# A gradient matmul on one core: three of the loads of G cut into 120 and 8 partitions

## The chip, the cores and the metric

The kernel runs on one core of a Trainium2 chip. The metric is the device time of one execution in microseconds (us), the median of several runs. A core has TensorE (PE, matmuls, with its weight loads shown as PEld), VectorE (DVE), ScalarE (ACT), GpSimd (POOL) and SyncE (SP), each working through its own instructions in order, and 16 DMA engines that move data between device memory and the core's on-chip memory of 128 partitions.

## The reference

```python
def reference(input, grad_output):        # input [16, 512, 1024] f32, grad_output [16, 512, 768] f32
    grad_weight = np.einsum('bmk,bmn->kn', input, grad_output)
    return grad_weight.astype(np.float32) # [1024, 768]
```

With batch and rows joined it is one product, X transposed times G, where X has 8192 x 1024 and G has 8192 x 768 elements.

## The kernel before

**Tiles.** The 8192 rows are cut into 64 slices of 128, and two slices make a pair `u`, from 0 to 31 (so the 5th, 9th and 13th pair are u = 4, 8 and 12). A pair's X is the tile `xp` (128 partitions, 2 x 1024, bf16), its G the tile `gp` (128 partitions, 2 x 768, bf16). The string `LOADS` (L12) gives each pair a kind. Kind `s` (the first seven and the last two pairs) gives two items that are multiplied plainly. Kind `P` (the 23 pairs between) gives one item for a scheme in the manner of Strassen, with seven products of half size in place of eight: DVE makes three sums of G halves (`ge`) and three of X halves (`xe`) and overwrites two halves of each tile in five instructions, `sum_g1` (L139), `sum_g2` (L144), `sum_x1` (L149), `sum_x2` (L153) and `sum_x3` (L158).

**Loads.** The loop at L108 to L126 issues all loads from POOL, in the order of the pairs. For u of 2 and above a pair is one transfer of G (L114) and one of X (L115). Both read f32 and write bf16. Partition p receives rows 2p and 2p + 1 of the pair, so each partition's data is one stretch of memory. The pairs live in 14 buffers (`PAIRS_HELD`), the sums in 9 (`SUMS_HELD`). POOL does nothing else; its queue holds just these transfers. The first two slices are loaded in f32 by SP and ACT and rounded there.

**Sums and products.** The output has quadrants A, B, C, D (each 512 x 384, as four blocks of 128 rows, q = 0 to 3). The five further products of the scheme are m, n, o, p and q. A product works in four banks of matmul memory, a slot; there are two slots, so two products are open at a time. A step such as `D9:2` in `ORDER` (L18 to L32) says: go on with product D up to its 9th item. A step with `!` closes the product afterwards: each bank is added to or copied into its sum in on-chip memory, by DVE (L356, L358), or by ACT (L354) for as many of the last banks as stand after the colon. ACT also carries a sum back into a bank before a product that it closes is opened again (L297, L324). The order on PE, DVE, ACT and POOL is the program's own order (`manual_schedule`, L84): `fill` hands out the DVE sums and, late in the kernel, the 20 `share` operations (L195) at the places that the numbers in `ORDER` name.

**What the steps around the loads need.** Products o and p read only halves that no sum overwrites, so their matmuls (L338) can begin when the pair's X and G have landed. q and n need `sum_x1` and `sum_g2`; m, D and A need other sums. The last P pair is u = 29, first used in step `5p23!1,0,1,1`. Pairs u = 30 and 31 are plain and used from `A38:0-q` on. The end, L389 to L403, stores the last block of D in two parts.

Of the kernel before, what the change touches and what calls it, by code (L numbers as in the profile page):

```python
# [9 lines left out]
P = 128  # L10
# [30 lines left out]
SUMS_HELD = 9  # L41

MERGED = 2


@with_exitstack
def kernel(
# [6 lines left out]
    nc = tc.nc  # L54
# [14 lines left out]
    G = grad_output.rearrange("b m n -> (b m) n")  # L69
# [38 lines left out]
    for u, kind in enumerate(LOADS):  # L108
        pool = pairs if u else head
        xp = pool.tile([P, 2, K], bf16, name="xp", tag="xp")  # L110
        gp = pool.tile([P, 2, N], bf16, name="gp", tag="gp")
        if u >= MERGED:
            rows = slice(2 * u * P, 2 * (u + 1) * P)
            nc.gpsimd.dma_start(out=gp, in_=G[rows, :].rearrange("(p m) n -> p m n", m=2))  # L114
            nc.gpsimd.dma_start(out=xp, in_=X[rows, :].rearrange("(p m) k -> p m k", m=2))  # L115
        for h in range(2):
            s = 2 * u + h
            if s > 0 and u < MERGED:
                nc.gpsimd.dma_start(out=gp[:, h, :], in_=G[s * P : (s + 1) * P, :])
            if s > 1 and u < MERGED:  # L120
                nc.gpsimd.dma_start(out=xp[:, h, :], in_=X[s * P : (s + 1) * P, :])
            if kind == "s":
                items.append(("s", xp[:, h, :], gp[:, h, :]))
        if kind == "P":
            items.append(("P", xp, gp))
        xg.append((xp, gp))  # L126
# [326 lines left out]
```

## Time and profile before

| | before |
|---|---|
| median of 3 runs | 162.97 us (162.89 to 163.16) |
| span of the profiled execution, first to last instruction | 161.1 us |
| PE busy | 157.0 us (97%) |
| DVE busy | 140.7 us (87%) |
| ACT busy | 117.9 us (73%) |
| POOL busy | 34.8 us (22%) |
| DMA queue of POOL's loads | 9360 packets, 28.64 MB written |
| read from device memory | 58.72 MB |

The times around the span (launch and end) are 1.87 us, the median less the span. Of the profile, the chain of work that ended last goes back from the last instruction to what released each; the groups give an operation's count, its busy time and the idle time before it with the releaser; the waits add up who waited for whom; the timeline lists instructions by start time, with the idle time before one and its releaser in brackets. "PEld" lines are weight loads, which run beside the matmul before them. A DMA transfer adds 16 to a count when it is done, one for each DMA engine, and the trace holds the time of each of the 16 increments and the queue, size and time of each DMA packet.

### The profile page before, as it was taken

Reading aid. Unit: us, or ns where it says so; the run is one execution under the profiler, and the core shown is the slowest. Engines: PE = TensorE matmul, PEld = TensorE weight load, DVE = VectorE, ACT = ScalarE, POOL = GpSimd, SP = SyncE. Lnnn points to the kernel's source line nnn. Section 1 sums busy time; section 2 is a strip of 40 time slices with the busy share of each in tenths; the row PEclk is TensorE's granted clock in tenths of the full one; section 3 lists DMA queues with packets and bytes.
Section 4 is the critical chain, followed back from the end, with each engine's and each line's share of the span. In section 5 each row is a group of like instructions: output and inputs, shape, how many; then the busy total and the mean of one; then the engine's idle time right before and its main releaser. Section 6 shows DMA issues by size and latency. Waiting matters only on the chain.

```text
span 161.1 us, 2769 instructions
## 1 busy us (share of the span) xinstructions
PE 157.0 (97%) x944; PEld 92.7 (58%) x944; DVE 140.7 (87%) x267; ACT 117.9 (73%) x278; POOL 34.8 (22%) x69
## 2 busy tenths in 40 slices
PE   8999999999999999999999999999999999999991
PEld 3365665556555565556655665556655665555561
DVE  0645888889799999999998999999989998999982
ACT  3735357545589899978998897997795667988730
POOL 7442222122222212222212222221222100000000
PEclk9999999999999999999999999999999999999999
DMA  5999999999999999999999999999999999900695
GB/s 176 297 210 214 213 214 216 212 215 212 214 213 212 212 212 216 212 213 211 214 212 217 212 215 213 213 213 213 213 212 213 213 214 213 202 21 0 239 354 191
DMA packets 12398, 33.40 MB, mean 207 GB/s; under 512 B 1376, under 2 KB 4192, under 8 KB 12384
## 3 DMA queue, kind: packets, MB, share of 16 engines
q0 software_dynamic: 9360, 28.64, 89.8%
q1 hardware_dynamic: 2592, 3.47, 6.2%
q10 hardware_dynamic: 432, 1.11, 1.8%
q8 instruction: 7, 0.11, 0.3%
q14 instruction: 7, 0.06, 0.1%
HBM read 58.72 MB, written 3.15 MB: 384 GB/s over the span
## 4 chain that ended last, share of the span: by engine, by line
PE 97%; DVE 0%; issue 0%
PE bank L338 94%; PE bank L97 3%; PE bank L393 0%; DVE acc L401 0%
## 5 line engine op out<-in xcount | busy, mean ns | idle before, releaser
L338 PEld LDWEIGHTS <-xp 128*128 128x128 bf16 x650 | 63.3, 98 | 44.4 <-DVE xp L212 1.5
L338 PE MATMUL bank<-gp,xp 128*128 128x384 bf16 x468 | 81.0, 327 | 0.0
L354 ACT COPY macc<-bank 128x384 f32<-128x384 f32 x91 | 39.3, 491 | 9.8 <-PE bank L338 9.4
L358 DVE TENSOR_TENSOR acc<-bank,acc 128x384 f32<-128x384 f32 x80 | 39.6, 550 | 5.2 <-PE bank L338 4.8
L338 PEld LDWEIGHTS <-xe 128*128 128x128 bf16 x276 | 26.9, 98 | 17.9 <-DVE xe L149 0.2
L354 ACT COPY acc<-bank 128x384 f32<-128x384 f32 x57 | 24.7, 484 | 13.9 <-PE bank L338 13.9
L297 ACT COPY bank<-macc 128x384 f32<-128x384 f32 x73 | 33.0, 493 | 1.6 <-DVE acc L358 0.9
L338 PE MATMUL bank<-ge,xp 128*128 128x384 bf16 x182 | 33.5, 326 | 0.0
L338 PE MATMUL bank<-gp,xe 128*128 128x384 bf16 x184 | 32.4, 326 | 0.0
L297 ACT COPY bank<-acc 128x384 f32<-128x384 f32 x47 | 21.5, 491 | 8.7 <-DVE acc L358 7.0
L115 POOL DMA_DIRECT2D xp<-in_input_dram x30 | 16.0, 532 | 52.1 <-DMA xp<-in_input_dram 28.9
L114 POOL DMA_DIRECT2D gp<-in_grad_output_dram x30 | 16.0, 533 | 38.1 <-PE bank L338 17.2
L358 DVE TENSOR_TENSOR macc<-bank,macc 128x384 f32<-128x384 f32 x35 | 18.0, 550 | 0.8 <-PE bank L338 0.8
L139 DVE TENSOR_TENSOR ge<-gp 128x1152 bf16<-128x1152 bf16 x23 | 17.3, 752 | 0.6 <-DMA gp<-in_grad_output_dram 0.5
L149 DVE TENSOR_TENSOR xe<-xp 128x1024 bf16<-128x1024 bf16 x23 | 15.8, 685 | 2.1 <-DMA xp<-in_input_dram 2.1
L195 DVE TENSOR_TENSOR acc<-acc,macc 128x768 f32<-128x768 f32 (+1 forms) x20 | 16.1, 871 | 0.0
L338 PE MATMUL bank<-ge,xe 128*128 128x384 bf16 x92 | 15.9, 326 | 0.0
L158 DVE TENSOR_TENSOR xp<-xp 128x1024 bf16<-128x1024 bf16 x23 | 15.7, 684 | 0.0
L144 DVE TENSOR_TENSOR gp<-gp 128x768 bf16<-128x768 bf16 x23 | 12.7, 554 | 0.5
L153 DVE TENSOR_TENSOR xe<-xp 128x512 bf16<-128x512 bf16 x23 | 9.6, 418 | 0.0
L356 DVE COPY acc<-bank 128x384 f32<-128x384 f32 x6 | 3.2, 555 | 3.2 <-PE bank L338 3.1
L212 DVE CAST gp<-gf 128x192 bf16<-128x192 f32 (+1 forms) x2 | 0.7, 330 | 4.3 <-DMA gf<-in_grad_output_dram 4.3
(20 smaller groups left out, 19.9 us busy)
## 6 DMA issues: line engine op xcount, KB each, us to landing
xp<-in_input_dram POOLq DMA_DIRECT2D x30, 512.0 KB, 16.8
gp<-in_grad_output_dram POOLq DMA_DIRECT2D x30, 384.0 KB, 16.7
out_dram<-acc SPq DMA_DIRECT2D x15, 192.0 KB, 2.4
xf<-in_input_dram ACTq DMA_DIRECT2D x2, 512.0 KB, 4.8
gp<-in_grad_output_dram POOLq DMA_DIRECT2D x3, 192.0 KB, 6.4
xp<-in_input_dram POOLq DMA_DIRECT2D x2, 256.0 KB, 7.7
gf<-in_grad_output_dram SPq DMA_DIRECT2D x2, 192.0 KB, 4.2
out_dram<-acc SPq DMA_DIRECT2D x1, 128.0 KB, 1.9
```

The costliest lines, as they stand in the source:

```text
L114: nc.gpsimd.dma_start(out=gp, in_=G[rows, :].rearrange("(p m) n -> p m n", m=2))
L115: nc.gpsimd.dma_start(out=xp, in_=X[rows, :].rearrange("(p m) k -> p m k", m=2))
L139: nc.vector.tensor_add(out=ge.rearrange("p a n -> p (a n)"), in0=g[:, 0 : 3 * NH], in1=g[:, NH : 4 * NH])
L144: nc.vector.tensor_sub(out=g[:, 0::3, :], in0=g[:, 0::3, :], in1=g[:, 2:0:-1, :])
L149: nc.vector.tensor_add(out=xe[:, 0:2, :].rearrange("p a k -> p (a k)"), in0=xp[:, 0, :], in1=xp[:, 1, :])
L153: nc.vector.tensor_add(out=extra[i][0][:, 2, :], in0=xp[:, 0, 0:KH], in1=xp[:, 1, KH:K])
L158: nc.vector.tensor_sub(out=x[:, 1:3, :], in0=x[:, 1:3, :], in1=x[:, 0::3, :])
L195: op(out=dst, in0=dst, in1=src)
L297: nc.scalar.copy(out=bank, in_=sum_of(p, q))
L338: nc.tensor.matmul(bank, stat, mov, start=opening and j == 0 and not carried, stop=close and j == len(items_now) - 1, skip_group_check=car ...
L354: nc.scalar.copy(out=dst, in_=bank)
L358: nc.vector.tensor_add(out=dst, in0=bank, in1=dst)
```

## The change

```diff
+SPLIT = (4, 8, 12)
...
         if u >= MERGED:
             rows = slice(2 * u * P, 2 * (u + 1) * P)
-            nc.gpsimd.dma_start(out=gp, in_=G[rows, :].rearrange("(p m) n -> p m n", m=2))
+            gsrc = G[rows, :].rearrange("(p m) n -> p m n", m=2)
+            for r in (slice(0, 120), slice(120, P)) if u in SPLIT else (slice(0, P),):
+                nc.gpsimd.dma_start(out=gp[r], in_=gsrc[r])
             nc.gpsimd.dma_start(out=xp, in_=X[rows, :].rearrange("(p m) k -> p m k", m=2))
```

For pairs u = 4, 8 and 12 the transfer of G becomes two: first partitions 0 to 119, then partitions 120 to 127, both from POOL and both ahead of the pair's X. All other transfers, the bytes, and the instructions of PE, DVE, ACT and SP stay as they are in the program.

## The prediction

> **What bounds the kernel now.** I read the chain that ended last first, then the strip of slices, the groups, the waits, and then two narrow stretches of the timeline.
>
> ```profile
> PEclk9999999999999999999999999999999999999999
> DMA  5999999999999999999999999999999999900695
> GB/s 176 297 210 214 213 214 216 212 215 212 214 213 212 212 212 216 212 213 211 214 212 217 212 215 213 213 213 213 213 212 213 213 214 213 202 21 0 239 354 191
> ```
>
> ```profile
> 0.78 4.42 PE bank L97 x6
> 5.20 2.25 PE bank L338 x12
> 7.45 0.01 issue
> 7.46 149.34 PE bank L338 x914
> ```
>
> The chain is TensorE from end to end: 914 matmuls in 149.34 us, 163.4 ns each, at the full granted clock. The middle distance between two matmul starts in the trace is 162.5 ns, so all waiting inside this piece is 149.34 − 914 × 0.1625 = 0.8 us, and half of it lies before 16 us. A change can hardly shorten this chain; it can only put holes into it. The strip shows the second thing: the DMA engines are full from the second slice until 142 us, at 213 GB/s. So loads run at their own ceiling, and a load's landing time is set by the bytes in front of it on its engine, not by when POOL issues it.
>
> How near are the two to each other? The waits of the whole run and the timeline around the last pair of kind P (the 30th) say so:
>
> ```profile
> POOL xp L115 <- DMA xp<-in_input_dram: 28.9, 17, 2.0
> ...
> DVE xe L149 <- DMA xp<-in_input_dram: 2.1, 4, 0.8
> ...
> PEld L338 <- DMA xp<-in_input_dram: 0.5, 2, 0.3
> ```
>
> ```profile
> 132.32 2.78 PE L338 MATMUL bank<-gp,xp 128*128 128x384 bf16 x16
> ...
> 133.60 0.69 DVE L149 TENSOR_TENSOR xe<-xp 128x1024 bf16<-128x1024 bf16 x1 [0.41 <-DMA xp<-in_input_dram]
> 133.62 1.25 PEld L338 LDWEIGHTS <-xp 128*128 128x128 bf16 x9 [0.23 <-DMA xp<-in_input_dram]
> ```
>
> At 133.6 us both DVE and the weight load stand waiting for the 30th pair's X (step p23). The completion count of that transfer is full at 133.58 us and the matmul starts at 133.63: a slack of 0.05 us. The matmuls stream through the wait without a hole (the PE line has none), so it costs nothing today; but any later landing goes straight into TensorE. By the same reckoning (first matmul on a pair less the last of its X's 16 completion increments) the slack is 0.36 us for the 9th pair (43.21 us), 0.45 for the 14th (64.85), 0.5 for the 23rd (103.88).
>
> The 16 increments of a transfer, one per DMA engine, also show which engine decides. Up to 20 us all 16 come within 0.35 us. Then one engine after the other falls back by about 1 us and stays back, after one 16 KB packet of the instruction queue each (893 to 999 ns; at 20.8, 42.1, 63.2, 82.9, 104.8, 124.3 us). At the 30th pair's X seven engines are 0.97 to 1.31 us behind the first, and the landing is theirs.
>
> **The change, part by part.**
>
> *Issue.* Three more L114 transfers of 0.53 us (the row "530/530/587" of that line) are 1.6 us of POOL. Each also takes its turn in POOL's wait for the transfer eight places earlier:
>
> ```profile
> 7.62 0.54 POOL L115 DMA_DIRECT2D xp<-in_input_dram  x1 [2.02 <-DMA gp<-in_grad_output_dram]
> 8.53 0.53 POOL L114 DMA_DIRECT2D gp<-in_grad_output_dram  x1 [0.37 <-DMA gp<-in_grad_output_dram]
> 9.78 0.53 POOL L115 DMA_DIRECT2D xp<-in_input_dram  x1 [0.72 <-DMA xp<-in_input_dram]
> 10.73 0.53 POOL L114 DMA_DIRECT2D gp<-in_grad_output_dram  x1 [0.42 <-DMA gp<-in_grad_output_dram]
> ```
>
> The 5th pair's X (issued at 9.78) moves to the next such turn, about 10.7 us, and everything behind it one place. It landed at 25.6 us, so 15 us of queued transfers cover a shift of 1 us; later issues sit 16.8 us ahead (the median to landing), and one turn there is about 2.1 us. Cost 0; without that cover it would be up to 2.1 us a split.
>
> *Waits.* A reader of these three G's has one more transfer to wait for. TensorE's sequencer has 23 separate waits of 51 ns on L338 today without a hole at most of them, and DVE the same kind, so I bound it by 0 and 0.05 us for each of three pairs. Queued behind it are, for the 5th pair, the matmuls of D9 (26.5 us, with the data there 0.9 us before); for the 9th and 13th sum_g1 on DVE and the four sums behind it, which TensorE waits for (the 13th pair's xe was ready 0.06 us before its matmul at 61.43). I take 0.
>
> *Engine load.* This decides. A G transfer is 0.393 MB at 213 GB/s, 1.85 us; its 128 rows are 8 on each engine, so a row costs its engine 0.23 us. No row of this trace shows a transfer of 120 or of 8 partitions. Bounds: all eight rows on the one engine that the 120 leave out (or 120 spread 7 and 8, and the eight filling up): nothing changes; all eight on one engine that already had eight: +1.85 us there. Nearest row: every load in the trace is spread evenly over 16 engines, so I take 15 engines with 8 rows each, one engine with none, and the last eight rows on eight engines, one each. Then each split makes eight engines 0.23 us later for good (the queue never empties, so nothing is caught up), and one engine 1.85 or 1.62 us earlier, which helps nobody: a landing is the last engine's. Each extra transfer also adds one 4-byte completion of 22 ns to every engine.
>
> After three splits 24 rows lie on 16 engines: an engine has three of them if the eight are the same engines each time (0.69 + 0.07 = 0.76 us), two if they rotate (0.46 + 0.07 = 0.53 us). With seven engines sharing the last place at the 30th pair, one with two or three rows is nearly certain among them. The landing moves by 0.53 to 0.76 us, less the slack of 0.05: 0.48 to 0.71. I take 0.55, since the last increments differ by 0.3 us and the engine with most rows need not be the very last.
>
> *On the way.* The 9th pair's X is up to 0.5 us late against 0.36, and DVE, which waits for it at 42.86 (0.76 us), passes that on to 61.43, where 0.06 is left: 0.1 to 0.4 us of hole. The 14th is 0.5 to 0.8 late against 0.45. These holes come first and the later wait shrinks by as much: they aren't added, the largest lateness counts. After 133.6 us only about 0.1 us of TensorE waiting is left that could swallow some of it, and the last two pairs land at 137.9 and 142.2 us, 4.5 us and more before their matmuls (143.6 and 146.7).
>
> **Sum.** Span 161.1 + 0.55 = 161.65; the median of the runs, 162.97, is 1.87 above the profiled span, so 163.5 us, +0.33%.
>
> Two rules of the Trainium skill, DMA: Bandwidth & Descriptors, weigh in. The section "Why a DMA increments its semaphore by 16 and not by 1" says that the engines used are the largest number up to 16 that divides the outer dimension (or, for some GpSimd copies, sixteenths rounded up): 15 for 120 rows, eight for 8, which would make it 163.5 to 163.7. The table "Rules for kernel authors" says that two transfers to disjoint partitions share the same engines and bring nothing; by that alone it would be 163.0. The increments above show why "nothing" may be too kind here. The page also calls engines 7 and 15 usually slower, which would speak for relieving one engine; in this trace no engine falls back steadily, they step back one after the other.
>
> **Rivals.**
>
> *No change.* The eight rows fill the engine that was left out, or fall on engines that are not among the last seven, or the 120 are spread in a way that evens out; then the change does not do what it says. Only the 0.07 us of completions against 0.05 of slack remain: 163.0, up to 163.25 with one row on a late engine. For: DVE and TensorE wait little for loads today. Against: seven of sixteen engines share the last place.
>
> *Faster.* The engine that is left out is the last one: just after 23 us one engine alone is 1.26 us behind, and the 5th pair's G would bring it in front; landings up to 34 us come some 0.6 us earlier. It decides only where TensorE has a hole that a load ends. From 16 us to the end all its holes together are 0.4 us, and those at 26.8 and 42.3 us follow copies of ACT. Gain at most 0.2 us: 162.8; for more, the runs without profiler would have to have holes that this trace hasn't.
>
> *Much slower.* The eight rows go to one engine that already carries eight: 1.85 us for one such split among the late engines, 5.5 if it is the same engine three times: 164.8 to 168.4. For: eight rows is what an engine gets in every transfer of this trace. Against: the even spread.
>
> **How the numbers follow.** Forecast 163.3 to 163.8: 0.55. No change: 0.26. Faster mechanism: 0.07 (with something outside this trace). Much slower: 0.12. A difference of 0.2% (0.33 us) is about what a measurement of this kernel can tell from no change; the border lies at 163.30. Slower: 0.53 + 0.12 = 0.65; same 0.28; faster 0.07. The range leaves out the much slower case and the far end of the faster one: 162.8 to 164.2.
>
> **What would show it.** Right: the wait of the weight load for X at the last combined pair grows from 0.23 us to 0.7 or more, with a hole in the matmuls of the same size; DVE's waits for X (2.1 us in all) grow; landing increments of pairs after the 13th end 0.5 to 0.8 us later; matmul durations stay. Wrong: no such hole though landings are later (slack misread), landings not later (rows spread otherwise), or a hole right after the 5th, 9th or 13th pair that ends on an extra wait.

## The result, and the profile after

The changed kernel takes **163.79 us** (163.73 to 163.89), the kernel before 162.97 us (162.89 to 163.16); the ratio is 1.0043, 95% interval 1.0023 to 1.0064. A second series, with 23 runs of the kernel before beside it, gives 1.0035 (1.0022 to 1.0048), which is 0.57 us (0.36 to 0.78). The change makes the kernel slower by about 0.4%.

The strips of the changed kernel have the same shape: the TensorE clock is full to the end of the matmuls, and the DMA engines are full until about 143 us.

```profile
PEclk9999999999999999999999999999999999999998
DMA  5999999999999999999999999999999999900695
GB/s 158 300 212 213 212 217 211 213 211 211 216 212 212 213 213 212 213 211 214 212 214 214 213 214 211 215 212 213 211 212 215 211 215 206 191 16 0 219 357 203
```

The chain that ended last is what differs (start, length, what). Before it was one unbroken row of matmuls; now it leaves TensorE at 79.7 us, runs through DVE and two loads of X, and comes back to TensorE at 134.64 us, after a load:

```profile
7.85 71.87 PE bank L341 x438
79.72 0.53 DVE macc L361
...
82.61 17.22 DMA xp<-in_input_dram
99.85 0.69 DVE xe L152
...
117.63 16.96 DMA xp<-in_input_dram
134.59 0.05 issue
134.64 23.17 PE bank L341 x141
```

The load issued at 117.63 us is the X of the 30th pair, the place that the prediction named. The chain counts that load from its issue, but the issue did not make it late: the first DMA engine was through with it at 127.41 us and the last at 134.59. The waits of the run (who, for whom, us in total, times, longest) and the timeline there:

```profile
DVE xe L152 <- DMA xp<-in_input_dram: 2.2, 5, 0.6
...
DVE ge L142 <- DMA gp<-in_grad_output_dram: 1.3, 4, 0.5
...
PEld L341 <- DMA xp<-in_input_dram: 1.2, 3, 0.6
...
PE bank L341 <- DMA xp<-in_input_dram: 0.2, 1, 0.2
```

```profile
131.80 2.60 PE L341 MATMUL bank<-gp,xp 128*128 128x384 bf16 x15
...
134.61 0.69 DVE L152 TENSOR_TENSOR xe<-xp 128x1024 bf16<-128x1024 bf16 x1 [0.41 <-DMA xp<-in_input_dram]
134.63 0.93 PEld L341 LDWEIGHTS <-xp 128*128 128x128 bf16 x7 [0.62 <-DMA xp<-in_input_dram]
134.64 1.15 PE L341 MATMUL bank<-gp,xp 128*128 128x384 bf16 x6 [0.24 <-DMA xp<-in_input_dram]
```

The weight load's wait has grown from 0.23 to 0.62 us, and TensorE itself now waits in step p23: the PE line carries a bracket that it did not have. Between two matmul starts there are 0.57 us instead of 0.16, so the hole is 0.40 us. Smaller holes of 0.10, 0.05 and 0.08 us stand at 100.3, 127.3 and 130.1 us; together 0.63.

One thing stands wrongly ahead of the prediction: of G, products o and p read just the two halves that `sum_g2` overwrites, and q and n read the other two. So the matmul on the 30th pair in step p23 needs `sum_g2` from DVE as well as X, and both counts are among its waits. These are the lines of `sum_g2`, before and after:

```profile
132.63 0.56 DVE L144 TENSOR_TENSOR gp<-gp 128x768 bf16<-128x768 bf16 x1
```

```profile
133.65 0.56 DVE L147 TENSOR_TENSOR gp<-gp 128x768 bf16<-128x768 bf16 x1
```

It ends at 133.19 and 134.21 us, about 0.4 us before X has landed (133.58 and 134.59), so X still decides here, but with no more room than that.

POOL's issue around the 5th pair went as predicted: the two transfers of G at 8.91 and 10.16 us, X one place later, and it landed at 25.76 us against 25.59 before.

```profile
8.91 0.54 POOL L117 DMA_DIRECT2D gp<-in_grad_output_dram  x1 [0.36 <-DMA gp<-in_grad_output_dram]
10.16 0.51 POOL L117 DMA_DIRECT2D gp<-in_grad_output_dram  x1 [0.71 <-DMA xp<-in_input_dram]
11.12 0.54 POOL L118 DMA_DIRECT2D xp<-in_input_dram  x1 [0.45 <-DMA gp<-in_grad_output_dram]
```

**Two numbers for each kernel.** The start of an execution scatters by some tenths of a us, so I compare traces by two things that don't count it in, both worked out from the instruction and completion records. *Length* is the time from the 41st matmul (at about 11 us) to the last one. *Spread* is the time between the 2nd and the 16th completion increment of the 30th pair's X (the first may belong to an engine that was left out; *lead* is how far that one is ahead of the 2nd).

| kernel | time against the kernel before | length, us | spread, us | lead, us |
|---|---|---|---|---|
| before, two profiles | 1 | 146.53, 146.47 | 1.31, 1.59 | 0.01, 0.03 |
| the change, two profiles | 1.0035 (1.0022 to 1.0048) | 147.14, 146.85 | 2.17, 2.05 | 5.0, 5.0 |
| 112 and 16 partitions | 1.0001 (0.9992 to 1.0010) | 146.53 | 1.35 | 0.06 |
| 5th pair only | 1.0012 (1.0003 to 1.0022) | 146.58 | 1.48 | 1.55 |
| 26th to 28th pair | 1.0034 (1.0021 to 1.0047) | 147.08 | 2.20 | 3.8 |
| 8 first, then 120 | 1.0032 (1.0022 to 1.0042) | 147.16 | 1.94 | 5.3 |
| six pairs | 1.0083 (1.0069 to 1.0097) | 147.75 | 2.87 | 4.5 |
| 31st and 32nd pair | 1.0006 (0.9996 to 1.0015) | 146.45 | 1.50 | 0.1 |
| the change, half of one G cut | 1.0000 (0.9991 to 1.0009) | 146.54 | 2.21 | 5.3 |
| before, half of one G cut | 1.0000 (0.9989 to 1.0011) | 146.45 | 1.54 | 0.04 |

### The profile page after: what moved, and what is told of

The parts are those of the page before. It is cut to its first block, busy times and chain, and to the rows that moved or that the text cites. A ratio compares the mean times of both kernels' runs of the same rounds, so it can differ in the third digit from the quotient of the medians.

```text
span 162.0 us, 2775 instructions
## 1 busy us (share of the span) xinstructions
PE 156.9 (97%) x944; PEld 92.4 (57%) x944; DVE 141.1 (87%) x267; ACT 117.9 (73%) x278; POOL 36.3 (22%) x72
## 2 busy tenths in 40 slices
DMA packets 12494, 33.40 MB, mean 206 GB/s; under 512 B 1472, under 2 KB 4288, under 8 KB 12480
## 4 chain that ended last, share of the span: by engine, by line
PE 60%; DMA 24%; DVE 12%; issue 1%; SPq 0%
PE bank L341 59%; DMA xp<-in_input_dram 21%; DMA gf<-in_grad_output_dram 3%; DVE macc L361 3%; DVE ge L142 2%; DVE acc L361 2%; DVE xe L152 2%; DVE gp L147 1%; DVE xp L161 1%; DVE xe L156 1%; PE bank L396 0%; DVE acc L404 0%; SPq L89 0%; DVE gp L215 0%
## 5 line engine op out<-in xcount | busy, mean ns | idle before, releaser
L117 POOL DMA_DIRECT2D gp<-in_grad_output_dram x33 | 17.6, 533 | 41.9 <-PE bank L341 18.2
```

Of the source, the lines that this page charges most:

```text
L117: nc.gpsimd.dma_start(out=gp[r], in_=gsrc[r])
```

## The experiments

**Theory (rows):** in each split the same eight DMA engines carry one row more and fall back by 0.23 us for good; the last of them sets the landing that TensorE waits for at the 30th pair. **Rivals:** the extra transfers themselves cost the time (issues, turns, waits); the damage is done early, on the tight DVE chain; the splits relieve the lagging engine; a fixed toll such as a late start.

### The change again, and the kernel before again

No edit.

> The changed kernel once more, for a narrow interval and a second profile. Rows theory (each split makes the same eight DMA engines one row, 0.23 us, and one completion, 0.02 us, later, and the last of them sets the landing of the 30th pair's X): 0.5 to 0.8 us over the kernel before, with a hole of about that size in the matmuls at the 30th pair. In the first profile of the changed kernel 0.39 us of the 1.02 us by which the matmuls end later was already there at 14 us, before any split pair is used. If that belongs to the change it shows here again; if it is chance of one execution, the start is as in the kernel before and only the holes stay.

> The kernel before, profiled a second time. Its first profile has the 30th matmul of the loads' part at 11.04 us, those of the kernels with three splits at 11.4 to 11.6, long before any split pair is used. If the start is chance of one execution, this profile may lie anywhere from 11.0 to 11.6, with no hole over 0.1 us at the 30th pair. If the late start belongs to the splits, it is at 11.0 to 11.1 again. Time: that of the kernel before, ratio 1.000 within 0.1%.

The change: 163.83 us against 163.16, with one hole of 0.39 us at the 30th pair and no other that the kernel before lacks. The kernel before, against itself: 0.9997 (0.9988 to 1.0006), no hole at the 30th pair; its weight loads there do not wait:

```profile
132.54 3.02 PEld L338 LDWEIGHTS <-xp 128*128 128x128 bf16 x19
...
133.71 0.69 DVE L149 TENSOR_TENSOR xe<-xp 128x1024 bf16<-128x1024 bf16 x1 [0.21 <-DMA xp<-in_input_dram]
```

The matmul that the expectations count as the 30th is the 41st of all. It starts at 11.57 us in this profile of the changed kernel, and in the second profile of the kernel before at 11.47 instead of 11.04. So the late start is chance of an execution, and 0.4 us of the 1.0 us between the first two profiles was no effect of the change.

### The same three splits, divided evenly

```diff
-            for r in (slice(0, 120), slice(120, P)) if u in SPLIT else (slice(0, P),):
+            for r in (slice(0, 112), slice(112, P)) if u in SPLIT else (slice(0, P),):
```

> The same three pairs split, but into partitions 0 to 111 and 112 to 127, so that both transfers divide evenly over 16 engines (7 rows and 1 row each). Issues, waits and completions are those of the change. Rows theory: no engine gets more than eight rows, only 0.07 us of completions, so 0 to 0.1 us over the kernel before. Transfers theory (the extra issue, its turn in POOL's queue and the extra wait of the readers cost the time): the same 0.5 to 0.8 us as the change.

1.0001 (0.9992 to 1.0010): no difference. The three extra issues, their turns in POOL's queue and the second wait of every reader are all in this kernel. Its timeline at the 30th pair has the row of matmuls unbroken, to within a hole of 0.08 us:

```profile
132.28 3.50 PE L341 MATMUL bank<-gp,xp 128*128 128x384 bf16 x20
...
133.82 1.58 PEld L341 LDWEIGHTS <-xp 128*128 128x128 bf16 x11 [0.30 <-DMA xp<-in_input_dram]
```

The transfers theory falls: what costs is that 120 and 8 don't divide by 16. (An uneven split also adds more 4-byte packets than this one; at 22 ns each they come to 0.07 us an engine over three splits.)

### One split, three late ones, six

```diff
-SPLIT = (4, 8, 12)
+SPLIT = (4,)                      # 5th pair only
+SPLIT = (25, 26, 27)              # 26th to 28th pair
+SPLIT = (4, 6, 8, 10, 12, 14)     # six pairs
```

> Only the 5th pair split, 120 and 8. Rows theory: the last engine is 0.25 us later from there on, less 0.05 us of slack at the 30th pair: 0.2 us over the kernel before. Rival (the engine left out is the one that lags at 23 us, and its relief helps the pairs behind it): 0 or a little below the kernel before.

1.0012, 0.2 us (0.05 to 0.36): the size of one row. The one profile, of an execution at the fast end (163.18 us), shows little of it: a hole of 0.08 us at the 30th pair, as in the kernel with 112 and 16, a length 0.08 above the mean of the kernel before, and a spread of 1.48 us, no wider than without a split. One engine is 1.55 us ahead, so an engine was relieved, but no landing comes earlier: at the 5th pair's X another engine is still the last one, 0.7 us behind all others, and that X lands at 25.74 us against 25.59 and 25.50 in the two profiles before.

> Three splits again, but of the 26th, 27th and 28th pair. Rows theory: what counts is how many extra rows the last engine has had when the 30th pair's X lands, not when it got them, so the time is that of the change, 0.5 to 0.8 us over the kernel before, in one hole at the 30th pair and none earlier. Rival (the early holes on the tight DVE chain around the 9th to 13th pair make the time): near the kernel before, at most 0.2 us over.

1.0034, the same as the change, although no pair before the 26th differs. So the early DVE chain is not where the time is lost. The count of holes was wrong: besides the one at the 30th pair (0.28 us) three of about 0.1 us stand at 125 to 127 us. The wait at the 30th pair:

```profile
134.64 1.58 PEld L341 LDWEIGHTS <-xp 128*128 128x128 bf16 x11 [0.50 <-DMA xp<-in_input_dram]
```

> Six splits: the 5th, 7th, 9th, 11th, 13th and 15th pair. Rows theory: six extra rows and completions, 6 x 0.25 = 1.5 us on the last engine, less 0.05: 1.4 to 1.6 us over the kernel before, twice the change, the larger part in holes already before 70 us because the DVE sums for the 13th pair had 0.06 us to spare. Rival (a fixed toll of the splits, such as a late start): 0.5 to 0.8 us as with three.

1.0083, 1.35 us (1.13 to 1.58): slightly under 1.4, and 2.4 times the three splits. The spread grows by 1.4 us over the mean of the five profiles without an uneven split before the 30th pair (1.46; they lie between 1.31 and 1.59), and with three splits by 0.65 in the mean of five profiles: 0.22 to 0.24 us a split, about one row each. That means the same eight engines each time; if they rotated, six splits would give at most three or four rows to one. The place of the holes was wrong: 0.28 at 61.6 us, as expected there, but then 0.13, 0.13, 0.09 and 0.29 between 75 and 101, and 0.29 at the 30th pair. This is the 13th pair's xe, and later pairs', coming too late for TensorE (the waits of the weight loads in this kernel):

```profile
PEld L341 <- DVE xe L152: 1.4, 3, 0.5
...
PEld L341 <- DMA xp<-in_input_dram: 1.0, 3, 0.5
PEld L341 <- DVE xp L161: 0.9, 3, 0.3
```

### The last two pairs

```diff
-SPLIT = (4, 8, 12)
+SPLIT = (30, 31)
```

> Only the last two pairs split, the 31st and 32nd, whose data lie 4.5 us and more ahead of their matmuls and behind the 30th pair in the queue. Rows theory: no hole, time of the kernel before within 0.1%. If the mere presence of uneven transfers costs (through the start or through a later execution), some of the 0.5 us of the change stays.

1.0006 (0.9996 to 1.0015), the same length as before, no hole. Uneven transfers behind the last tight landing cost nothing that can be measured. A fixed toll of the size of the change is out.

### More room for the loads

In the first of these kernels, with the change, and in the second, without a split (`SPLIT = ()`):

```diff
-                nc.gpsimd.dma_start(out=gp[r], in_=gsrc[r])
+                if u == 16:
+                    nc.gpsimd.memset(gp[:, :, 0:NH], 0.0)
+                    nc.gpsimd.dma_start(out=gp[r][:, :, NH:], in_=gsrc[r][:, :, NH:])
+                else:
+                    nc.gpsimd.dma_start(out=gp[r], in_=gsrc[r])
```

> The change, and in the 17th pair only the left half of G is loaded, POOL fills the other half with zeros (part of the product is left out). That takes 0.9 us off the load stream for all engines from there on, more than the three rows' 0.75. Rows theory: the 30th pair's X lands as early as in the kernel before or earlier, the hole of 0.4 us at the 30th pair is gone, the time is 0 to 0.25 us over the kernel before (what early holes before the 17th pair and the start leave). Transfers theory (waits or issues cost): the time of the change, 0.5 to 0.8 us over.

> No split, but in the 17th pair only the left half of G is loaded and POOL fills the other half with zeros (part of the product is left out): loads land about 0.9 us earlier from there on. If TensorE has no hole left that a load ends, earlier loads bring nothing: the time of the kernel before within 0.1%, and that of the change with the same cut. If relief of the loads could have made the kernel faster (the rival in which the split helps), 0.2 us or more below the kernel before.

With the change: 1.0000. The spread is that of the change (2.21 us), the lead too, but the 30th pair's X lands 0.8 to 0.9 us earlier (133.67 us against 134.59 and 134.43), and the hole is gone; the weight loads do not wait there at all:

```profile
132.27 3.58 PE L345 MATMUL bank<-gp,xp 128*128 128x384 bf16 x21
132.44 3.02 PEld L345 LDWEIGHTS <-xp 128*128 128x128 bf16 x19
...
133.69 0.69 DVE L156 TENSOR_TENSOR xe<-xp 128x1024 bf16<-128x1024 bf16 x1 [0.30 <-DMA xp<-in_input_dram]
```

So the uneven engines cost time only through the landing. Without a split: 1.0000 as well, though X of the 30th pair lands 0.98 us before its matmul. So from the 17th pair on earlier loads can't make this kernel faster. For the earlier pairs, where the faster rival lies, the kernel with one split shows it: no landing came earlier, and TensorE's holes there (0.14 us at 27 and 0.15 at 43 us) stayed as they were.

### The eight rows first

```diff
-            for r in (slice(0, 120), slice(120, P)) if u in SPLIT else (slice(0, P),):
+            for r in (slice(0, 8), slice(8, P)) if u in SPLIT else (slice(0, P),):
```

> The same three pairs, but partitions 0 to 7 first and then the 120 partitions 8 to 127. If the engines are dealt out by the place of a row in its transfer, the same engine stays out and the same eight get a row more: 0.5 to 0.7 us over the kernel before, with one increment about 5 us ahead of the others. If a partition belongs to a fixed engine, nothing is uneven (every engine gets its own eight rows): the time of the kernel before.

1.0032, with one engine 5.3 us ahead: the effect is that of the change. Rows are dealt to engines by their place in the transfer, not by the partition that they go to.

```profile
134.54 1.58 PEld L341 LDWEIGHTS <-xp 128*128 128x128 bf16 x11 [0.59 <-DMA xp<-in_input_dram]
134.55 1.96 PE L341 MATMUL bank<-gp,xp 128*128 128x384 bf16 x11 [0.20 <-DMA xp<-in_input_dram]
```

## Why the prediction was right

It forecast 163.5 us, +0.33%, for one reason: later landings on eight engines. Measured were +0.43% (0.23 to 0.64) and +0.35% (0.22 to 0.48), and the reason held in each of the tests that could have broken it. That 0.55 us came so near the 0.57 measured is in part luck, since several terms were off and their errors nearly cancel.

- *The bound.* Right. TensorE has no time to give: half a G less to load leaves the time at 1.0000 (0.9989 to 1.0011).
- *Issue and waits, taken as 0.* Right: 1.0001 (0.9992 to 1.0010) with both in place, 0.16 us at most.
- *The spread of rows.* The nearest row (every load lies evenly on 16 engines) gave the right end of bounds 0 and 1.85 us: one engine left out (lead 1.55 us after one split, 5.0 after three), eight with one row more. Left open was whether the eight are the same. They are; so the term is 0.69 us for the rows, the upper one of the two, and the spread shows 0.65.
- *Completions.* Mis-sized. The profile counts 96 more small packets for three splits (1472 against 1376 under 512 B), 32 a split and not 16; with 112 and 16 partitions it is 48 (1424). At 22 ns that is 0.13 us an engine over three splits instead of 0.07, if they lie evenly.
- *The slack of 0.05 us.* Misread. In every profile in which TensorE or its weight load waits for this landing, the matmul starts 0.05 us after it: that is the time from the last increment to the start, not a reserve. The reserve of the kernel before was 0 in its first profile and 0.31 − 0.05 = 0.26 us in the second, since the start of the matmuls and that of the loads scatter against each other. A landing that rows (0.65 to 0.69) and completions (0.07 to 0.13) make 0.7 to 0.8 us later and a reserve of 0 to 0.26 give 0.45 to 0.8 us; lengths are 0.35 to 0.64 us longer, the timed runs 0.36 to 0.78.
- *Holes on the way.* Forecast at 43 to 65 us; in both profiles of the change none is there, and 0.26 us at 61.6 when the eight rows went first. Whether the delay reaches TensorE there differs from profile to profile; why stays open. These holes do not add, as forecast: the late splits cost the same.
- *The signs.* The hole came (0.40 and 0.39 us), and the distance of two matmul starts stayed at 162.5 ns. The wait of the weight load grew from 0.23 to 0.62 and 0.61 us, short of the 0.7 that was named, and DVE's waits for X did not grow: 2.2 and 2.0 us against 2.1.
- *How engines fall back.* Read too simply. Besides the six 16 KB packets, the second instruction queue (q14) has five packets of 8 KB (322 ns each, at 32.6, 40.7, 84.9, 87.4 and 93.1 us) before the 30th pair, and engines fall back by less than 1 us too: one by 0.5 to 0.8 us between 32 and 35 us, while no 16 KB packet ran from 20.8 to 42.1. Nothing in the sum rests on this.
- *The sum's base.* The first profile started 0.4 us earlier than the second of the same kernel, so a base taken from one profile carries that much by chance; the median of 162.97 was low as well (163.16, 163.07 and 163.06 in later series).

Of the rivals, "no change" would have needed an even spread; the kernel with 112 and 16 is that case, and gives it. "Much slower" needed all eight rows on one engine, which did not happen: the spread grew by 0.65 us. "Faster" needed the relief to reach the last engine and a hole for it to fill; with one split no landing came earlier. On the rules of the Trainium skill, DMA: Bandwidth & Descriptors: the section "Why a DMA increments its semaphore by 16 and not by 1" has 15 engines for 120 rows and eight for 8, and the lead and the spread agree. The row on disjoint partitions in "Rules for kernel authors" says that such a split brings nothing; here an even split brings nothing (1.0001) and an uneven one costs 0.2 us (0.05 to 0.36) for one and 1.35 us for six.

## What to carry to other kernels

In this kernel, whose DMA engines are always full, loads of 120 and 8 partitions left eight of 16 engines one row behind for the rest of the stream, and every landing is the last engine's; where loads run like this, count rows per engine, not bytes. Whether that costs anything was decided here mostly at one place, the tightest landing that the matmuls wait for: splits behind it were free, and three splits before it cost the same early or late (1.0035 and 1.0034). With six, sums of DVE for earlier pairs came too late as well. That relief of an engine helps only where it is the last one and the bounding engine has a hole to fill is an argument; the runs show only that it did not help here.

## What the runs showed that was not expected

- The lead of the engine that is left out does not grow without end: 5.0 us after three splits, and 4.5 us at the 30th pair after six (4.8 at the 14th), where six times the 1.55 us of one split would make 9.3. It must then stand idle at times. The trace with six splits suggests how: the lead reaches 7.1 us there and drops more than once, for example at the 13th pair's X, which POOL issued at 47.97 us, just after the transfer eight places earlier was full (47.68). The leading engine's increment for it came at 54.13 us, 4.5 us after the one before, where 2.5 us is usual for an X. So POOL seems to have issued too late for it; no run tested that.
- An uneven split adds 32 small packets to the queue, an even one 16. What the other 16 are stays open.
- The start of one and the same kernel moved by 0.4 us between two profiles, and the reserve at the tightest landing by 0.26 us, with time medians that differ by only 0.1 to 0.2 us.
